# SSD and gMLP layers of a streaming encoder: GpSimd's products move to VectorE, and two tiles of v get banks of their own

## The chip, the core and the metric

The kernel runs on one core of one Trainium2 chip. The metric is the device time of one execution in microseconds (us). The median of three timed runs of the kernel before is 1218.1 us (1212.23 to 1220.72). A difference of about 1% is the least that can be told from no change here.

## The reference

One step of a two-layer streaming encoder, width 1024, on 640 tokens: 512 of one new stream (four tiles of 128 tokens) and 128 of eight running streams (16 tokens each, the fifth tile). All arithmetic is fp32 accurate.

Layer 0 is a Mamba-2 SSD mixer. RMSNorm, then a projection to z, x, B, C and dt; a causal depthwise convolution of width 4 with SiLU on x, B and C; 32 heads of 64 channels in 8 groups that share B and C:

```python
    def step(h, inp):
        la = jnp.cumsum(dtc * a_g, axis=1)
        decay = jnp.exp(jnp.where(causal, seg, -jnp.inf))
        y_in = jnp.einsum('btsg,btsgr,bsgr,bsgrp->btgrp', cb, decay, dtc, xc)
        y_st = jnp.einsum('btgn,bgrpn->btgrp', cc, h) * jnp.exp(la)[..., None]
        w_in = jnp.exp(last[:, None] - la) * dtc
        h_new = h * jnp.exp(last)[..., None, None] + jnp.einsum('bsgn,bsgr,bsgrp->bgrpn', bc, w_in, xc)
```

Then a D skip, a SiLU(z) gate with a group RMSNorm and the output projection, added to the residual. Layer 1 is a gMLP: a projection to u, v and z, GELU on u and v, a LayerNorm of v, for each of 8 head groups a 128x128 position-mixing matrix on v, `u * (W_s v + b) * SiLU(z)`, and an output projection. A final RMSNorm closes it. Outputs are y, the last convolution rows, the new SSM states, and v of the running streams.

## The kernel before

**Precision.** Every fp32 operand of a large matmul is split in a high part (H, rounded) and a low part (L, the rest); three matmuls H·H, H·L and L·H make one product. Splits are made by a ScalarE copy and a VectorE subtraction.

**The weight stream of layer 0.** Weights come in units of 128x1024 fp32 (512 KB). `Stream.fill` (L106) issues on GpSimd's queue the transfer of a unit into `wh` (L112). `Stream.low` (L99) makes the low part of the unit before: ScalarE writes -H into `wl` (L102), and GpSimd issues a second transfer of the same weights that is added to it (L103). `next()` is called before a unit's matmuls and issues the low part of the unit two ahead and the high part of the unit three ahead; each of the two tiles has four buffers. So GpSimd's queue holds, for each unit, L103 and then L112: L103 waits for ScalarE's L102, that waits for the landing of the transfer issued one unit before, and a new L112 stands behind it.

**The SSD groups.** A loop runs over 8 groups (L447). The units of a middle group g (1 to 6), in TensorE's order, are x0, x1, B, C, z0, two of `a_w_out` (o, o, the output projection of group g-1), and z1. x0, x1, B and C are each followed by `conv_tile` (L409), whose last steps are a tanh on ScalarE (L430) and a product on VectorE (L431). `to_tokens` (L467) transposes x to tokens and makes `xdt` (x·dt, VectorE, L481) and `xw` (xdt·decay, GpSimd, L483). `old_states` (L575) reads the running streams' states h0 and then scales them by their decay, eight products on GpSimd (L589). `cb_prompt` (L594) makes `CBm`, the masked C·B (L598); its buffer is shared with `hl`, the split of xw and B that is sent out to DRAM as `dhl`. `mask(i)` (L631) multiplies the four decay tiles E of the group by CBm (L633): three on VectorE and one, the last, on GpSimd; in the last group two and two. `pair(i)` (L635) is the y of two heads. `some(5, 10)` (L704) are the last five of the ten pieces of the output projection, evicted by VectorE (L688). After `pair(1)` come `gate(0)`, `new_states` and the unit z1, then `gate(1)` and in the next group x0 and x1. `gate(i)` (L674) makes tanh (L677), two products (L678, L679), a split (L301 on ScalarE, L302 on VectorE) and a square (L682 on ScalarE); L719 adds the squares of both, and `pss_` (L684) sums them on TensorE during the second half of unit x1. Group 0 has no output projection, and group 7 does the one of group 6 in `L713` to `L718`.

**Order.** In layer 0 TensorE and GpSimd run in the order in which the program is written. VectorE, ScalarE and SyncE run in an order that a planner sets when the program is built; each still runs in order. In layer 1 all engines run in the written order.

**The head of layer 1.** `v_tiles` (L827) makes v in four blocks of 512 columns; tiles 0 to 4 of a block take PSUM banks of the pools `o` and `m` in rotation (L828), ScalarE evicts with GELU (L843), VectorE takes the statistics (L846). `v_norm(t)` (L849) scales a tile by its LayerNorm factors, two ScalarE passes over 1024 columns (L858). Tiles 0 to 2 are scaled in the last block; tiles 3 and 4 in the first step of the loop over 16 feature tiles f (L1015 and L1020). In a step, seven products (`prod`, L957) of 12 matmuls each go to three banks pa (`m`), pb (`in`) and pc (`m`), with evictions between them (L1014 to L1048), and `mix` (L1040) mixes the positions of v. Later work of a step (`gate1`, `gate2`, `new_v`) is put in a list that `then()` takes from between the products of the next step.

Of the kernel before, what the change touches and what calls it, by code (L numbers as in the profile page):

```python
# [12 lines left out]
ALU = mybir.AluOpType  # L13
# [5 lines left out]
TT = 5  # L19
# [21 lines left out]
def hybrid_step(ctx: ExitStack, tc: tile.TileContext, xin, xT0, cst, wdt, cache, wA, wAo, h0in, wB, wBv, wBo,  # L41
                lnwb, spc, bsp, nwb, y_out, nconv_out, sspP_out, sspS_out, v_out):
    nc = tc.nc
    V, S, G, T = nc.vector, nc.scalar, nc.gpsimd, nc.tensor
# [102 lines left out]
    def norm_first(zp, rb):  # L147
        xH, xL = norm_tiles()
        xt = zp.tile([P, KD, NT], F32, name="xt")
        nc.sync.dma_start(out=csb[0][:, :8], in_=cst[:, :8])  # L150
        nc.sync.dma_start(out=xt[:, 0, :], in_=xT0[0])
        dw = zp.tile([P, KD, HEADS], F32, name="dw")
        nc.sync.dma_start(out=dw, in_=wdt)
        dHL = zp.tile([P, KD, 2, HEADS], F32R, name="dHL")
        S.copy(out=dHL[:, :, 0], in_=dw)
        V.tensor_tensor(out=dHL[:, :, 1], in0=dw, in1=dHL[:, :, 0].bitcast(F32), op=ALU.subtract)
        W = stream.first(2, lambda i: [nc.sync.dma_start(out=xt[:, k, :], in_=xT0[k]) for k in ((1,), range(2, KD))[i]])
        nc.sync.dma_start(out=csb[0][:, 8:], in_=cst[:, 8:NCST1])
        acc = [zp.tile([P, NT], F32, name=f"sqa{i}") for i in range(2)]
        for k in range(KD):  # L160
            w = C("nw0")[:, k:k + 1]
            S.activation(xH[:, k, :], xt[:, k, :], AF.Identity, scale=w)
            V.scalar_tensor_tensor(xL[:, k, :], xt[:, k, :], w, xH[:, k, :].bitcast(F32), ALU.mult, ALU.subtract)
        stream.fill(1)
        stream.low()
        warm = ps_op.tile([P, 512], F32, name="warm", tag="op")
        for _ in range(13):
            mm(warm[:, :P], ones, ones)
        pdt, px0 = [[pool.tile([P, 512], F32, name="pin", tag=tag)[:, :b - a] for a, b in HALVES]
                    for pool, tag in ((ps_y, "y"), (ps_in, "in"))]  # L170

        def dt_step(k):
            lw = dHL[:, k].rearrange("p a h -> p (a h)")
            for (a, b), o in zip(HALVES, pdt):
                mm(o[:64], lw, xH[:, k, a:b], start=(k == 0), stop=False)
                mm(o[:64], lw, xL[:, k, a:b], start=False, stop=(k == KD - 1))

        dt_step(0)
        for k in range(KD):
            if k + 1 < KD:  # L180
                dt_step(k + 1)
            for h in range(2):
                in_proj_step(W, (xH, xL), px0[h], h, k)
        dtT = zp.tile([64, NT], F32, name="dtT")
        for (a, b), o in zip(HALVES, pdt):
            S.copy(out=dtT[:, a:b], in_=o[:64])
        for k in range(KD):
            if k < 2:
                S.activation(acc[k], xt[:, k, :], AF.Square, scale=1.0 / 32)
            else:  # L190
                S.activation(xt[:, k, :], xt[:, k, :], AF.Square, scale=1.0 / 32)
                (V if k % 2 else G).tensor_tensor(out=acc[k % 2], in0=acc[k % 2], in1=xt[:, k, :], op=ALU.add)
        V.tensor_tensor(out=acc[0], in0=acc[0], in1=acc[1], op=ALU.add)
        rs = small.tile([P, TT], F32, name="rs0")

        def fin():
            pms = ps_m.tile([P, TT], F32, name="pms", tag="m")
            for t in range(TT):
                mm(pms[:, t:t + 1], acc[0][:, t * P:(t + 1) * P], ones[:, 0:1])
            V.tensor_copy(rs, rsqrt(pms, EPS, TT))  # L200
            ptd = ps_m.tile([P, TT, HEADS], F32, name="ptd", tag="m")
            for t in range(TT):
                mm(ptd[:, t, :], dtT[:, t * P:(t + 1) * P], C("sel")[:64])
            return ptd

        def half(a, b):
            pb = ps_m.tile([P, 512], F32, name="pb", tag="m")
            for t in range(a // P, b // P):
                dg = zp.tile([P, P], F32, name="dg", tag="dg", bufs=2)
                V.tensor_scalar(dg, ident, rs[:, t:t + 1], None, ALU.mult)  # L210
                mm(pb[:, t * P - a:(t + 1) * P - a], ones, dg)
            S.copy(out=rb[:, a:b], in_=pb[:, :b - a])

        return (xH, xL), px0, rs, fin, half
# [77 lines left out]
    def bank(b, n):  # L292
        return {"o": ps_op, "y": ps_y, "m": ps_m}[b].tile([P, 512], F32, name=n, tag={"o": "op"}.get(b, b))
# [29 lines left out]
    with ExitStack() as ca:  # L323
# [35 lines left out]
        for d in (15, 13, 11, 9, 7, 5, 3):  # L359
# [17 lines left out]
                        in1=C("blk").rearrange("p (b o) -> p b o", o=1).broadcast_to([P, 8, HEADS]), op=ALU.mult)  # L377
# [69 lines left out]
        for g in range(GROUPS):  # L447
# [19 lines left out]
            def to_tokens(j, ta, tb):  # L467
                n = tb - ta
                tp = ps_y.tile([P, n, P], F32, name="tp", tag="y")
                for t in range(ta, tb):  # L470
                    T.transpose(out=tp[:, t - ta, :], in_=xcs[j][:, t * P:(t + 1) * P], identity=ident)
                if j == 2:
                    S.copy(out=Bt[:, ta:tb, :], in_=tp)
                    if tb == TT:
                        stack_sample()
                else:
                    xv = tp.rearrange("p t (r q) -> p t r q", q=64)
                    h_ = slice(4 * g + 2 * j, 4 * g + 2 * j + 2)
                    r_ = slice(2 * j, 2 * j + 2)
                    dv = dt[:, ta:tb, h_].rearrange("p t (r o) -> p t r o", o=1).broadcast_to([P, n, 2, 64])  # L480
                    V.tensor_tensor(out=xdt[:, ta:tb, r_], in0=xv, in1=dv, op=ALU.mult)  # L481
                    ev = esu[:, ta:tb, h_].rearrange("p t (r o) -> p t r o", o=1).broadcast_to([P, n, 2, 64])
                    G.tensor_tensor(out=xw[:, ta:tb, r_], in0=xdt[:, ta:tb, r_], in1=ev, op=ALU.mult)  # L483

# [88 lines left out]
            def old_states():  # L575
                Cs = Cf[:, 512:640].rearrange("p (q e j) -> p q e j", q=4, e=2)
                for e in range(2):
                    V.tensor_copy(cz[:, :, e, e, :], Cs[:, :, e, :])
                yq = ps_op.tile([P, 4, 64], F32, name="yq", tag="op")
                for e in range(2):  # L580
                    for q in range(4):
                        mm(yq[32 * q:32 * q + 32], cz[:, q, e].rearrange("p a j -> p (a j)"),
                           h0[q // 2][:, (2 * q + e) % 4], start=(e == 0), stop=(e == 1))
                V.tensor_tensor(out=yss, in0=yq, in1=elt[:, hsl].rearrange("p (r o) -> p r o", o=1).broadcast_to([P, 4, 64]),
                                op=ALU.mult)
                for b in range(8):
                    hv = h0[b // 4][:, b % 4]
                    ev = etot[:, 4 + b, hsl].rearrange("p (r o) -> p r o", o=1).broadcast_to([P, 4, 64])
                    G.tensor_tensor(out=hv, in0=hv, in1=ev, op=ALU.mult)  # L589


            CBm = wk.tile([P, TT, P], F32, name="CBm", tag="CBm", bufs=1)
# [37 lines left out]

            def mask(i):  # L631
                for e in range(2):
                    (G if i and (last or e) else V).tensor_tensor(out=Es[2 * i + e], in0=Es[2 * i + e], in1=CBm, op=ALU.mult)  # L633

            def pair(i):  # L635
                Ms = [Es[2 * i], Es[2 * i + 1]]
# [153 lines left out]
    with ExitStack() as cb_:  # L790
# [34 lines left out]


        def v_tiles(Wv, vb, ts, mid=lambda: None, unit=lambda u: None):  # L827
            pss = [bank("oomm"[(vb * TT + t) % 4], "pv") for t in ts]  # L828
            for u in range(4):
                wH, wL = Wv[u]  # L830
                for t, ps in zip(ts, pss):
# [121 lines left out]
        def then(n=1):  # L953
            for _ in range(min(n, len(later))):
                later.popleft()()
# [32 lines left out]
        for g in range(GROUPS):  # L988
# [9 lines left out]
            for i in range(2):  # L998
# [13 lines left out]
                c5 = wk.tile([P, HT], F32, name="c5", tag="c5", bufs=1)  # L1012
                prod(pa, "m1", True)
                S.copy(out=c1, in_=pa)  # L1014
                if f == 0:  # L1015
                    v_norm(3)
                then()
                prod(pb, "m6", True)
                V.tensor_tensor(out=uu[:, hi], in0=pb, in1=c1, op=ALU.add)
                if f == 0:  # L1020
                    v_norm(4)
                then()
                pc = ps_m.tile([P, 512], F32, name="pqc", tag="m")[:, :HT]
                prod(pc, "m5", True)
# [1 line left out]
                then()  # L1026
                prod(pa, "m2", False)
                S.activation(uu[:, lo], pa, AF.Gelu)
                then()
                prod(pb, "m7", False)  # L1030
                V.tensor_tensor(out=zz[:, hi], in0=pb, in1=c5, op=ALU.add)  # L1031
                then(9)
                prod(pc, "m3", False)
                V.tensor_tensor(out=uu[:, hi], in0=pc, in1=uu[:, hi], op=ALU.add)
# [11 lines left out]
                    mix()  # L1046
                prod(pb, "m4", False)
                V.tensor_tensor(out=zz[:, lo], in0=pb, in1=c1, op=ALU.add)  # L1048
                if not f:
                    mix()  # L1050
                th = wk.tile([P, NT], F32, name="thb", tag="thb", bufs=1)
                S.activation(th, zz, AF.Tanh, scale=0.5)
                qb = wk.tile([P, 2, P], F32, name="qb", tag="qb", bufs=1)
# [23 lines left out]
                    G.tensor_tensor(out=lwb[:, 0], in0=lwb[:, 0], in1=lwb[:, 1], op=ALU.add)  # L1077
                    nc.sync.dma_start(out=v_out[:, f // 4, vs], in_=lwb[:, 0])

                positions()  # L1080
                later.extend([gate1, gate2, new_v])

        oo = bp.tile([P, TT + 2, D], F32, name="oo", tag="v")
        fnw_sb = oo[:, TT]
# [131 lines left out]
```

## Time and profile before

| what | value |
|---|---|
| median of 3 timed runs | 1218.1 us (1212.23 to 1220.72) |
| the profiled execution | 1213.09 us |
| its span, first to last instruction | 1211.3 us |
| mean granted TensorE clock | 0.954 of 2.4 GHz |
| TensorE busy | 1061.1 us (88%) |
| VectorE busy | 838.5 us (69%) |
| ScalarE busy | 451.7 us (37%) |
| GpSimd busy | 200.0 us (17%) |

In the rows PE is TensorE's matmuls, PEld its weight loads, DVE VectorE, ACT ScalarE, POOL GpSimd, SP SyncE. Times are us from the span's start unless they are marked ns. `out<-in` names the tiles that an instruction writes and reads, `L302` is line 302 of the kernel. In a timeline the bracket is the idle time of the engine before the instruction and what ended it. Layer 0 lasts until about 730 us, the rest is layer 1.

### The profile page before, as it was taken

What the parts mean: (1) busy time and instruction counts of PE and PEld (TensorE: products, weight loads), DVE (VectorE), ACT (ScalarE), POOL (GpSimd) and SP (SyncE); (2) the same over time, 40 slices, a digit from 0 to 9 for tenths busy, and PEclk for the clock granted to TensorE, in tenths of its full rate; (3) what the DMA queues carried; (4) which work ended last, traced back from release to release, by engine and by line L of the source; (5) the groups of instructions that cost most, each with busy time, mean ns of one, the idle gap of its engine ahead of it and who ended that gap; (6) DMA issues with size and microseconds to landing.
All of it is one profiled execution on the core that took longest, in us unless ns stands there. A gap on an engine that the chain in (4) does not pass through costs nothing.

```text
span 1211.3 us, 16913 instructions
## 1 busy us (share of the span) xinstructions
PE 1061.1 (88%) x6387; PEld 950.9 (79%) x6387; DVE 838.5 (69%) x1565; ACT 451.7 (37%) x897; POOL 200.0 (17%) x278
## 2 busy tenths in 40 slices
PE   8996887888888887887888888999799999999996
PEld 7885777777777677776777766888789899889985
DVE  6667774675665674665665677664788888888886
ACT  5443515315215215215215224334533343333343
POOL 3123221222232132132132500000000000000000
PEclk9998888989988999998989998999999999999999
DMA  8577647557656656656647551222141333224222
GB/s 271 119 223 197 165 121 200 132 120 200 146 120 192 145 122 189 152 125 180 146 127 187 136 178 64 70 70 78 48 126 62 96 99 104 67 84 126 75 68 87
DMA packets 66001, 157.93 MB, mean 130 GB/s; under 512 B 10080, under 2 KB 28768, under 8 KB 65920
## 3 DMA queue, kind: packets, MB, share of 16 engines
q0 software_dynamic: 18144, 66.07, 24.3%
q1 hardware_dynamic: 47776, 90.78, 24.1%
q8 instruction: 51, 0.84, 0.3%
q14 instruction: 30, 0.25, 0.1%
HBM read 139.96 MB, written 16.86 MB: 129 GB/s over the span
## 4 chain that ended last, share of the span: by engine, by line
PE 29%; issue 23%; DVE 18%; DMA 14%; POOL 8%; ACT 7%; SPq 0%; POOLq 0%; ACTq 0%; DVEq 0%
PE pv L69 8%; PE pop L69 8%; DMA wh<-wA 4%; DMA wh<-wAo 4%; PE pqb L69 3%; DMA dhl<-hl 3%; POOL h L589 3%; DVE wf L751 3%; PE pin L69 2%; PE pqc L69 2%; PE pqa L69 2%; POOL wl L103 2%; POOL wh L112 2%; DVE acc L424 2%; DVE h L967 1%
## 5 line engine op out<-in xcount | busy, mean ns | idle before, releaser
L69 PE MATMUL pin<-xH,wh 128*128 128x384 f32 (+1 forms) x768 | 256.6, 334 | 22.2 <-DVE xp L416 17.7
L69 PE MATMUL pin<-xH,wl 128*128 128x384 f32 (+1 forms) x768 | 244.8, 319 | 1.4 <-DMA wl<-wA 1.4
L69 PE MATMUL pin<-xL,wh 128*128 128x384 f32 (+1 forms) x768 | 245.0, 319 | 0.0
L69 PEld LDWEIGHTS pin<-xH,wh 128*128 128x128 f32 x768 | 153.1, 199 | 32.4 <-issue 24.4
L102 ACT ACTIVATE wl<-wh 128x1024 fp32r<-128x1024 f32 x63 | 66.5, 1056 | 264.6 <-DMA wh<-wA 142.8
L69 PEld LDWEIGHTS pin<-xH,wl 128*128 128x128 f32 x768 | 152.3, 198 | 2.0 <-DMA wl<-wA 2.0
L69 PEld LDWEIGHTS pin<-xL,wh 128*128 128x128 f32 x768 | 153.5, 200 | 0.2
L69 PE MATMUL pop<-wh,yHL 128*128 128x512 f32 x320 | 104.8, 409 | 19.3 <-DVE CBm L598 10.0
L424 DVE SCALAR_TENSOR_TENSOR acc<-xp,cw,acc 128x664 f32<-128x664 f32 x96 | 91.8, 956 | 37.6 <-ACT acc L419 36.1
L69 PE MATMUL pop<-wf,yHL 128*128 128x512 f32 x480 | 115.3, 397 | 1.4 <-DVE h L967 0.7
L69 PEld LDWEIGHTS pop<-wf,yHL 128*128 128x128 f32 x480 | 89.2, 188 | 25.4 <-DVE h L967 3.7
L751 DVE TENSOR_TENSOR wf<-raw,wf 128x512 fp32r<-128x512 f32 x128 | 86.6, 686 | 28.1 <-ACT wf L750 27.1
L103 POOL DMA_DIRECT2D wl<-wA x47 | 41.5, 883 | 348.4 <-ACT wl L102 315.7
L750 ACT CAST wf<-raw 128x512 fp32r<-128x512 f32 x128 | 76.5, 616 | 56.8 <-PE pop L69 27.2
L69 PEld LDWEIGHTS pop<-wh,yHL 128*128 128x128 f32 x320 | 58.0, 190 | 36.3 <-DVE CBm L598 12.1
L431 DVE SCALAR_TENSOR_TENSOR xc<-xc,acc 128x512 f32<-128x512 f32 x64 | 28.7, 489 | 61.0 <-ACT xc L430 60.8
L69 PE MATMUL pqa<-xH,wf 128*128 128x320 f32 x256 | 63.7, 318 | 5.3 <-ACT v L843 3.2
L688 DVE SCALAR_TENSOR_TENSOR h<-pop,rr,h 128x512 f32<-128x512 f32 x80 | 59.4, 746 | 10.3 <-PE pop L69 9.9
L69 PE MATMUL pv<-wh,xL 128*128 128x512 f32 x160 | 63.4, 396 | 2.4 <-DVE xL L235 2.4
L69 PE MATMUL pqb<-tf,wf 128*128 128x320 f32 x384 | 63.0, 313 | 2.0 <-DVE zz L1031 2.0
L69 PE MATMUL pv<-wh,xH 128*128 128x512 f32 x160 | 63.5, 397 | 0.1
L69 PE MATMUL pv<-wl,xH 128*128 128x512 f32 x160 | 63.1, 395 | 0.0
(223 smaller groups left out, 2067.9 us busy)
## 6 DMA issues: line engine op xcount, KB each, us to landing
wh<-wA POOLq DMA_DIRECT2D x47, 512.0 KB, 7.2
wl<-wA POOLq DMA_DIRECT2D x47, 512.0 KB, 5.6
raw<-wB SPq DMA_DIRECT2D x32, 512.0 KB, 3.7
E<-laD SPq DMA_DIRECT2D x32, 320.0 KB, 8.5
h<-h0in SPq DMA_DIRECT2D x16, 512.0 KB, 5.0
out_sspS<-h SPq DMA_DIRECT2D x16, 512.0 KB, 5.4
wh<-wAo POOLq DMA_DIRECT2D x16, 512.0 KB, 6.5
wl<-wAo POOLq DMA_DIRECT2D x16, 512.0 KB, 5.7
```

The costliest lines, as they stand in the source:

```text
L69: T.matmul(out, lhsT=lhsT, rhs=rhs, start=start, stop=stop, **kw)
L102: S.activation(L, H.bitcast(F32), AF.Identity, scale=-1.0)
L103: G.dma_start(out=L, in_=src, accum_op=ALU.add)
L112: G.dma_start(out=H, in_=src)
L424: V.scalar_tensor_tensor(acc[:, 0:664], xp[:, k:k + 664], cw[:, 4 * ft + k:4 * ft + k + 1], acc[:, 0:664], ALU.mult, ALU.add)
L431: V.scalar_tensor_tensor(o, o, 1.0, a, ALU.add, ALU.mult)
L589: G.tensor_tensor(out=hv, in0=hv, in1=ev, op=ALU.mult)
L688: V.scalar_tensor_tensor(h1[:, t, dsl], ps, rg[:, t:t + 1], h1[:, t, dsl], ALU.mult, ALU.add)
L750: S.copy(out=t[:, 0], in_=src)
L751: V.tensor_tensor(out=t[:, 1], in0=src, in1=t[:, 0].bitcast(F32), op=ALU.subtract)
L967: V.scalar_tensor_tensor(h1[:, t, dsl], ps, 0.5, h1[:, t, dsl], ALU.mult, ALU.add)
```

## The change

Five things:

- The three sums of squares in `norm_first` (L192) that GpSimd made are made by VectorE.
- `xw` (L483), the eight state decays of a group (L589) and all masks (L633) are made by VectorE. GpSimd has only the issues of weight transfers left in layer 0.
- Tiles 3 and 4 of v take the two banks of the pool `y`, the others `o`, `o` and `m`, the same in every block.
- `v_norm(3)` and `v_norm(4)` are written two products later each: after the GELU of pa's second use, and after L1031.
- The mixing of step f = 0 is no longer at the end of its own step but in the list of later work, with the rest of its positions, so it runs between the products of step 1.

```diff
@@ norm_first @@
-                (V if k % 2 else G).tensor_tensor(out=acc[k % 2], in0=acc[k % 2], in1=xt[:, k, :], op=ALU.add)
+                V.tensor_tensor(out=acc[k % 2], in0=acc[k % 2], in1=xt[:, k, :], op=ALU.add)
@@ to_tokens @@
-                    G.tensor_tensor(out=xw[:, ta:tb, r_], in0=xdt[:, ta:tb, r_], in1=ev, op=ALU.mult)
+                    V.tensor_tensor(out=xw[:, ta:tb, r_], in0=xdt[:, ta:tb, r_], in1=ev, op=ALU.mult)
@@ old_states @@
-                    G.tensor_tensor(out=hv, in0=hv, in1=ev, op=ALU.mult)
+                    V.tensor_tensor(out=hv, in0=hv, in1=ev, op=ALU.mult)
@@ mask @@
-                    (G if i and (last or e) else V).tensor_tensor(out=Es[2 * i + e], in0=Es[2 * i + e], in1=CBm, op=ALU.mult)
+                    V.tensor_tensor(out=Es[2 * i + e], in0=Es[2 * i + e], in1=CBm, op=ALU.mult)
@@ v_tiles @@
-            pss = [bank("oomm"[(vb * TT + t) % 4], "pv") for t in ts]
+            pss = [bank("oommyy"[t + 1 if t > 2 else t], "pv") for t in ts]
@@ the loop over feature tiles @@
                 prod(pa, "m1", True)
                 S.copy(out=c1, in_=pa)
-                if f == 0:
-                    v_norm(3)
                 then()
                 prod(pb, "m6", True)
                 V.tensor_tensor(out=uu[:, hi], in0=pb, in1=c1, op=ALU.add)
-                if f == 0:
-                    v_norm(4)
                 then()
...
                 prod(pa, "m2", False)
                 S.activation(uu[:, lo], pa, AF.Gelu)
+                if f == 0:
+                    v_norm(3)
                 then()
                 prod(pb, "m7", False)
                 V.tensor_tensor(out=zz[:, hi], in0=pb, in1=c5, op=ALU.add)
+                if f == 0:
+                    v_norm(4)
                 then(9)
...
                 V.tensor_tensor(out=zz[:, lo], in0=pb, in1=c1, op=ALU.add)
-                if not f:
-                    mix()
...
-                positions()
-                later.extend([gate1, gate2, new_v])
+                if f:
+                    positions()
+                    later.extend([gate1, gate2, new_v])
+                else:
+                    later.extend([gate1, lambda m=mix, p=positions: (m(), p()), gate2, new_v])
```

## Rows read from the trace of the kernel before

**Rows 1.** Busy time of PE, PEld, DVE, ACT, POOL from 253 to 342, clock, DMA
```profile
253.00:342.00 89.00, 74.37 (x477) 66.65 (x476) 54.77 (x103) 31.06 (x68) 22.26 (x31) 0.94 0.62 154
```

**Rows 2.** Waits of TensorE, all of the span: total us, times, longest
```profile
PE yB L69 <- POOL E L633: 29.5, 6, 4.9
...
PE pin L69 <- DVE xp L416: 17.7, 5, 4.7
...
PE pop L69 <- DVE y L654: 4.7, 1, 4.7
...
PE pqa L69 <- ACT v L843: 3.2, 1, 3.2
...
PE pqb L69 <- DVE zz L1031: 2.0, 1, 2.0
```

**Rows 3.** Chain that ended last, 240 to 345: start, us, what
```profile
253.29 4.56 POOL h L589 x8
...
263.61 8.38 issue
```

**Rows 4.** Timeline of GpSimd, from the last pop of group 2 on
```profile
252.69 0.55 POOL L112 DMA_DIRECT2D wh<-wA  x1 [11.82 <-PE pop L69]
...
262.17 0.89 POOL L103 DMA_DIRECT2D wl<-wA  x1 [2.83 <-ACT wl L102]
```

**Rows 5.** Timeline of VectorE in the same stretch
```profile
253.93 6.09 DVE L302 SCALAR_TENSOR_TENSOR yHL<-y,csb,yHL 128x640 fp32r<-128x640 f32 x1
...
275.09 0.88 DVE L302 SCALAR_TENSOR_TENSOR yHL<-y,csb,yHL 128x640 fp32r<-128x640 f32 x1 [0.90 <-ACT yHL L301]
...
284.45 0.82 DVE L719 TENSOR_TENSOR y<-y 128x640 f32<-128x640 f32 x1 [8.01 <-ACT y L682]
...
327.37 0.69 DVE L598 TENSOR_TENSOR CBm<-cb,csb 128x512 f32<-128x512 f32 x1 [4.18 <-DMA dhl<-hl]
```

**Rows 6.** Groups by shape, whole span: busy us, mean ns, idle before
```profile
L302 DVE SCALAR_TENSOR_TENSOR yHL<-y,csb,yHL 128x640 fp32r<-128x640 f32 x16 | 45.4, 2837 | 13.1 <-ACT yHL L301 13.1
```

**Rows 7.** Timeline of ScalarE in the same stretch
```profile
260.06 0.74 ACT L682 ACTIVATE y<-y 128x640 f32<-128x640 f32 x1 [6.64 <-DVE yHL L302]
260.70 1.04 ACT L102 ACTIVATE wl<-wh 128x1024 fp32r<-128x1024 f32 x1
...
282.74 1.06 ACT L102 ACTIVATE wl<-wh 128x1024 fp32r<-128x1024 f32 x1 [7.68 <-DMA wh<-wA]
```

**Rows 8.** The transfer issued at 252.69: KB, us from issue to landing
```profile
wh<-wA POOLq DMA_DIRECT2D x1, 512.0 KB, 3.8
```

**Rows 9.** Products of the same shapes on VectorE
```profile
L633 DVE TENSOR_TENSOR E<-E,CBm 128x640 f32<-128x640 f32 x23 | 19.9, 875 | 0.1
...
L481 DVE TENSOR_TENSOR xdt<-tp,dt 128x512 f32<-128x512 f32 x16 | 10.9, 684 | 0.6 <-DMA laD<-laT 0.4 <-PE tp L471 0.2
...
L567 DVE TENSOR_TENSOR hs<-hs,etot 128x256 f32<-128x256 f32 x24 | 10.3, 428 | 4.1 <-ACT hs L564 3.8
```

**Rows 10.** TensorE from 258 to 264: length, busy (matmuls), granted clock, DMA share, GB/s
```profile
258.00:264.00 6.00, 4.61 (x26) 0.52 0.09 8
```

**Rows 11.** The products on GpSimd, by shape
```profile
L589 POOL TENSOR_TENSOR h<-h,etot 128x256 f32<-128x256 f32 x64 | 37.3, 651 | 1.0 <-PE yq L69 0.9
L483 POOL TENSOR_TENSOR xw<-xdt,esu 128x512 f32<-128x512 f32 x16 | 24.7, 1546 | 57.4 <-DVE xdt L481 57.4
L633 POOL TENSOR_TENSOR E<-E,CBm 128x640 f32<-128x640 f32 x9 | 15.2, 1688 | 3.7 <-issue 3.7
```

**Rows 12.** Timeline of VectorE in group 1: the C·B mask
```profile
148.06 0.68 DVE L598 TENSOR_TENSOR CBm<-cb,csb 128x512 f32<-128x512 f32 x1
```

**Rows 13.** Timeline of GpSimd in group 7, after the two masks
```profile
692.86 0.90 POOL L103 DMA_DIRECT2D wl<-wAo  x1
```

**Rows 14.** Timeline of ScalarE in group 7
```profile
685.57 1.06 ACT L102 ACTIVATE wl<-wh 128x1024 fp32r<-128x1024 f32 x1 [6.67 <-DMA wh<-wAo]
...
701.51 1.06 ACT L102 ACTIVATE wl<-wh 128x1024 fp32r<-128x1024 f32 x1 [7.44 <-DMA wh<-wAo]
```

## The prediction

> **What bounds the kernel now.** I read the busy times by stretch first. In a middle SSD group of 89 us TensorE works 74.4, VectorE 54.8 and GpSimd 22.3 us [rows 1]: no engine is full, so layer 0 is bound by waits, not by an engine. The waits of TensorE name them: six times yB waits 4.9 us for the one mask that GpSimd makes (29.5 us), five times unit x1 waits for VectorE's L416 (17.7 us), once a pop waits 4.7 us [rows 2]. The chain that ended last then passes, in each group, through GpSimd: the eight state decays, the mask, and the issues of the weight stream with the landings between them [rows 3]. All this has one form at the six ends of groups 1 to 6; I take that of group 2. T is 252.69, when the last pop frees a buffer and GpSimd can issue the high part of x1 [rows 4].
>
> Until T GpSimd stands 11.8 us at that issue [rows 4], and the decays and the mask are written behind it. So the mask, whose inputs are long there, comes only after the issue, the 4.6 us of the decays [rows 3] and its own time, and TensorE waits for it. In the same 6 us VectorE's split L302 takes 6.09 us, while the same instruction takes 0.88 at 275.09 [rows 5]. Over the kernel, 16 of them take 45.4 us [rows 6]; 16 at 0.88 are 14.1, the excess of 31.3 is six times 5.2. L302 holds the square L682 on ScalarE until 260.06, and behind that in ScalarE's order stands L102, the low part of x1, at 260.70 = T + 8.0 [rows 7]. Its weights had landed at T + 3.8 [rows 8]. From L102 the stream goes on: GpSimd's next two issues at T + 9.5 [rows 4], landing, L102, issue. The third such L102 comes at 282.74, waiting 7.7 us for its landing [rows 7]; behind it stands the square of gate(1), behind that L719 on VectorE (8.0 us idle, 284.45) [rows 5], and behind that L416, which frees the bank for x1's second half. So between T and T + 33 it is the stream, not TensorE, that sets the pace, and TensorE's wait for the mask is partly slack.
>
> **The boundary of two groups, six times.** The mask on VectorE costs 0.87 [rows 9], is written ahead of five evictions and is ready some 7 us before T: yB's wait goes. L302 is back at 0.88, so the square ends at about T + 2.9, and L102 of x1 can start when its weights land, at T + 3.8 plus a few tenths. It moves from T + 8.0 to T + 4.0. TensorE gains more, 4.9 us of wait, and also some of what it lost at a granted clock of 0.52, the lower of its two levels (1.2 GHz), after that wait [rows 10], but it runs into the stream: x1's second half waits for the third L102, which moved by 4.0 only. So the wait of L416 grows from 3.4 to some 5.5 us, and what the boundary gains is 4.0 us. Ends: 0 (the landings eat it) and 4.9 plus the 3.5 us of L416's wait (17.7 over 5), if that goes too. I take 4.0, since every later step hangs on that L102. Six times: 24.0.
>
> **What VectorE gets.** For each group eight decays like L567 at 0.43, 3.4 us; one mask (two in group 7); and four pieces of xw like L481, two at 0.68 and two smaller ones, at most 2.7 us [rows 9]. On GpSimd they took 0.65, 1.69 and 1.55 each [rows 11]. The decays are ready once the old states are read, just before L598, the C·B mask. There VectorE stands 4.2 us for the transfer of `hl` that holds the shared buffer [rows 5]: 3.4 fits in the hole, and costs nothing. Without that cover, 3.4 us would go straight onto the masks and pops of the group. In group 1 there is no hole, L598 runs without idle before it [rows 12]: a loss of 0 to 4.3. Against it, GpSimd's issues in groups 0 and 1 no longer stand behind xw and the decays (0 to 4). I take 0 for both together. The second mask of pair 1 stands before the evictions of the late pops; they run behind TensorE by less than a piece there, and I take 0, at most 0.9 a group. xw lies beside waits of VectorE for ScalarE's tanh, taken as 0, at most 2.7 a group. The three sums of squares: 0, from -1 to +1; VectorE has them done when TensorE comes to the sum.
>
> **Group 7.** GpSimd makes two masks there, and the issue L103 at 692.86 stands behind them [rows 13], though its L102 ended at 686.6 [rows 14]. The next high part then lands at 701.5, ScalarE waits 7.4 us for it [rows 14], with gate(0)'s split behind it, and in the end a pop waits 4.7 us [rows 2]. Without the masks the issue goes 5.9 us earlier. The gain ends at TensorE's wait: 4.7, ends 2 and 5.9.
>
> **The head of layer 1.** Product m1 waits 3.2 us for the GELU of tile 4, whose bank it takes [rows 2]. The new banks remove that, but m2 must wait for ScalarE's copy of pa, which stays where it is: TensorE gets there earlier and waits longer, gain 0. m4 waits 2.0 us for L1031 [rows 2], held by the scaling of tiles 3 and 4 on ScalarE; later scaling gives up to 2.0, and step 1 pays part of it. In the first block tiles 3 and 4 now wait until the transposes of the norm have left the `y` banks: a loss of up to 2. I take a gain of 1, ends -3 and +4.
>
> **The sum.** 24.0 + 0 + 4.7 + 1.0 = 29.7. Against the profiled execution, 1213.1 - 29.7 = 1183.4 us. The median of the runs stands 5.0 above that execution, so for a median **1188 us**, chance 0.62.
>
> **A rule beside the trace.** The L302 rows say that one VectorE instruction stood through nine instructions of GpSimd. The Trainium skill (SBUF — State Buffer, Who interferes with whom) says that a VectorE instruction with two SBUF inputs and a GpSimd instruction that reads SBUF exclude each other, and that the second to issue blocks until the first finishes. The trace agrees that they exclude each other, but it shows a wait of 5.2 us, not one of a single GpSimd instruction. By the letter of that rule only the first 0.65 us of the wait were GpSimd's.
>
> **Rivals.**
> 1. *The long L302 has another cause, and stays.* Then L102 of x1 stays at T + 8.0, TensorE loses in front of x1 what it gains at yB, and the boundaries give 0: 1213.1 - 4.7 - 1.0 = 1207.4, as a median 1212. For it: the wait is longer than one GpSimd instruction. Against it: it is there only beside GpSimd's products, six times the same 5.2 us. Chance 0.07.
> 2. *The landings eat half.* With TensorE 5 us earlier, SyncE's loads of states and decays fall earlier on the stream, and the later landings (7.7 us of idle at 282.74 [rows 7], against 3.8 us alone [rows 8]) stretch. At 2 us a boundary: 1213.1 - 12 - 4.7 - 1 = 1195.4, median 1200. Chance 0.17.
> 3. *Both waits go.* The planner lets the square of gate(1) go ahead of the third L102, so x1 does not wait: 29.5 + 17.7 + 4.7 + 1 = 52.9, median 1165. For it: VectorE's, ScalarE's and SyncE's order is planned anew. Against it: nothing in the change alters what that square and that L102 wait for. Chance 0.08.
> 4. *Slower: VectorE becomes the bound of the SSD groups.* Place: the stretch from the conv products to the masks. The added 3.4 + 0.9 + 2.7 = 7.0 us a group lie on its path, over 8 groups 56, against the gain of 29.7: 1213.1 + 26 = 1239, median 1244. It decides where the hole ahead of L598 is under 3.4 us, or the planner puts the decays behind L598 in all groups. For it: group 1 has no hole. Against it: 54.8 of 89 us busy, of which 5.2 was standing in L302. Chance 0.06.
>
> **How the numbers follow.** 1% of 1218 is 12, about what can be told from no change, so faster is below 1206 and slower above 1230. Forecast (0.62), rival 3 (0.08) and most of rival 2 (0.12 of 0.17) are faster: 0.82. Rival 1 and the rest of 2 are within: 0.12. Rival 4: 0.06. The range reaches from 1170, which takes in the upper ends of the forecast's terms, to 1213, with rivals 1 and 2, and leaves out 3 and 4.
>
> **What would show it.** L302 at 0.88 in all 16; no wait of yB for a mask; L102 of x1 at about T + 4.0; the wait of x1 for L416 grown to 5 us or more at five or six boundaries; L598 still idle before it in groups 2 to 7, with the decays in that hole. The forecast is wrong if the third L102 comes no earlier after T than 30.0 us, if the decays stand behind L598, or if L416's wait shrinks.

## The result and the profile after

The changed kernel takes 1198.3 us (median of 4 runs, 1195.4 to 1201.4) against 1217.4 for the kernel before on the same chip: a ratio of 0.985 [0.980, 0.989], 19 us less. The forecast was 1188, inside 1170 to 1213. The profiled execution has a span of 1198.9 against 1211.3; of these 12.4 us layer 0 gives 18.2 (the first matmul on `pv` moves from 734.0 to 715.8) and layer 1 takes 5.9 back. These two are single executions, and lie closer together than the medians.

What the prediction said of instructions is there. VectorE's split, the evictions ahead of it and the product behind T, from the timeline of VectorE after (T is now 253.66), and the group by shape:

```profile
254.25 0.75 DVE L688 SCALAR_TENSOR_TENSOR h<-pop,rr,h 128x512 f32<-128x512 f32 x1 [0.54 <-PE pop L69]
254.92 0.88 DVE L302 SCALAR_TENSOR_TENSOR yHL<-y,csb,yHL 128x640 fp32r<-128x640 f32 x1
```
```profile
L302 DVE SCALAR_TENSOR_TENSOR yHL<-y,csb,yHL 128x640 fp32r<-128x640 f32 x16 | 14.1, 880 | 8.4 <-ACT yHL L301 8.4
```

All 16 are short, against 45.4 us [rows 6]. The stream follows on ScalarE, L102 being the negation that waits for a landing:

```profile
257.26 1.06 ACT L102 ACTIVATE wl<-wh 128x1024 fp32r<-128x1024 f32 x1 [0.70 <-DMA wh<-wA]
267.96 1.06 ACT L102 ACTIVATE wl<-wh 128x1024 fp32r<-128x1024 f32 x1 [9.63 <-DMA wh<-wA]
...
273.18 0.74 ACT L682 ACTIVATE y<-y 128x640 f32<-128x640 f32 x1 [0.95 <-DVE yHL L302]
281.03 1.06 ACT L102 ACTIVATE wl<-wh 128x1024 fp32r<-128x1024 f32 x1 [7.11 <-DMA wh<-wA]
```

The first L102 comes at T + 3.6 (before T + 8.0 [rows 7]), but the third at T + 27.4 (before T + 30.1): 1.7 of the 4.4 us are lost on the way, in waits of 9.6 and 7.1 for landings. In the mean of the six boundaries 2.9 of 4.3 us are lost by then. The square of gate(1), L682, now stands ahead of the third L102, not behind it. The waits of TensorE, whole span, after:

```profile
PE tp L471 <- DVE xc L431: 44.0, 12, 6.3
PE pin L69 <- DVE xp L414: 34.0, 13, 4.8
PE pqa L69 <- ACT c L1014: 7.2, 2, 5.5
...
PE tp L471 <- DVE xdt L481: 5.8, 1, 5.8
PE pqc L69 <- DVE c L1021: 4.9, 4, 2.4
...
PE yB L69 <- DVE E L633: 2.0, 6, 0.4
...
PE pop L69 <- DVE y L654: 0.4, 1, 0.4
```

The same two groups that lead this list, in the kernel before:

```profile
PE tp L471 <- DVE xc L431: 27.4, 15, 6.6
...
PE pin L69 <- DVE xp L414: 3.8, 1, 3.8
```

yB's 29.5, L416's 17.7 and group 7's 4.7 [rows 2] are gone or nearly so (2.0, none and 0.4); in their place L414 has grown by 30 us and xc by 17, the evictions and the conv of the next tile.

### The profile page after: what moved, and what is told of

The parts are those of the page before. It is cut to its first block, busy times and chain, and to the rows that moved or that the text cites. A ratio compares the mean times of both kernels' runs of the same rounds, so it can differ in the third digit from the quotient of the medians.

```text
span 1198.9 us, 16816 instructions
## 1 busy us (share of the span) xinstructions
PE 1063.2 (89%) x6387; PEld 958.0 (80%) x6387; DVE 830.3 (69%) x1673; ACT 453.9 (38%) x897; POOL 110.5 (9%) x170
## 4 chain that ended last, share of the span: by engine, by line
issue 49%; PE 25%; DVE 13%; POOL 7%; ACT 4%; DMA 2%; SPq 0%; POOLq 0%; ACTq 0%; DVEq 0%
PE pv L69 9%; PE pop L69 5%; PE pqb L69 4%; POOL wh L112 4%; POOL wl L103 3%; PE pqa L69 3%; PE pqc L69 3%; DVE wf L751 2%; DVE h L967 1%; DMA wh<-wA 1%; DVE uu L1062 1%; ACT wf L750 1%; DVE thb L1061 1%; DVE uu L1065 1%; ACT yHL L298 1%
## 5 line engine op out<-in xcount | busy, mean ns | idle before, releaser
L69 PE MATMUL pin<-xH,wh 128*128 128x384 f32 (+1 forms) x768 | 259.7, 338 | 35.6 <-DVE xp L414 34.0
L102 ACT ACTIVATE wl<-wh 128x1024 fp32r<-128x1024 f32 x63 | 66.7, 1059 | 248.6 <-DMA wh<-wA 184.9
L424 DVE SCALAR_TENSOR_TENSOR acc<-xp,cw,acc 128x664 f32<-128x664 f32 x96 | 87.0, 906 | 92.8 <-ACT acc L419 91.5
L751 DVE TENSOR_TENSOR wf<-raw,wf 128x512 fp32r<-128x512 f32 x128 | 86.5, 686 | 29.4 <-ACT wf L750 28.3
L471 PE MATMUL tp<-csb,xc 128*128 128x128 f32 x120 | 27.9, 345 | 53.3 <-DVE xc L431 44.0
L471 PEld LDWEIGHTS tp<-csb,xc 128*128 128x128 f32 x120 | 18.7, 177 | 58.5 <-DVE xc L431 34.2
```

The lines of the kernel that those rows point to most:

```text
L69: T.matmul(out, lhsT=lhsT, rhs=rhs, start=start, stop=stop, **kw)
L102: S.activation(L, H.bitcast(F32), AF.Identity, scale=-1.0)
L424: V.scalar_tensor_tensor(acc[:, 0:664], xp[:, k:k + 664], cw[:, 4 * ft + k:4 * ft + k + 1], acc[:, 0:664], ALU.mult, ALU.add)
L751: V.tensor_tensor(out=t[:, 1], in0=src, in1=t[:, 0].bitcast(F32), op=ALU.subtract)
```

## The experiments

Twelve kernels, each against the kernel before. T is the issue that waited for the last pop, as in the prediction; the first and last of six are listed, a period is a fifth of their distance. Differences in us that the text gives for a kernel are its ratio's, times the median of before (1211.5 to 1217.4). Layer 1 runs from the first matmul on `pv` to the last on `pqa`.

| kernel | ratio to before [95%] | first, last T | period | third L102 after T, mean | layer 1 begins, lasts |
|---|---|---|---|---|---|
| before | 1 | 162.63, 611.64 | 89.8 | 29.6 | 734.0, 430.9 |
| the change | 0.985 [0.980, 0.989] | 165.39, 602.39 | 87.4 | 28.2 | 715.8, 436.8 |
| 1 masks alone | 0.996 [0.993, 0.999] | 161.56, 612.81 | 90.3 | 31.8 | 731.1, 430.3 |
| 2 decays alone | 0.991 [0.987, 0.996] | 162.32, 600.20 | 87.6 | 28.6 | 720.2, 430.9 |
| 3 masks and decays | 0.978 [0.974, 0.982] | 161.50, 594.23 | 86.5 | 28.1 | 708.0, 429.9 |
| 4 head alone | 1.006 [1.003, 1.008] | 166.09, 617.60 | 90.3 | 29.4 | 738.4, 436.6 |
| 5 change without head | 0.982 [0.978, 0.986] | 163.24, 600.05 | 87.4 | 28.2 | 714.2, 430.0 |
| 6 (3) with banks | 0.978 [0.974, 0.982] | 161.82, 595.00 | 86.6 | 28.1 | 708.4, 431.4 |
| 7 (6) with own memory | 0.982 [0.978, 0.985] | 165.28, 599.75 | 86.9 | 28.2 | 715.2, 431.9 |
| 8 (3), negation on GpSimd | 1.008 [1.005, 1.011] | 166.65, 624.41 | 91.6 | 30.2 (on GpSimd) | 745.2, 430.8 |
| 9 before, issue later | 1.018 [1.015, 1.022] | 170.51, 643.03 | 94.5 | 28.1 | 758.9, 430.0 |
| 10 (3) without stores | 0.962 [0.958, 0.966] | 163.74, 574.42 | 82.1 | 24.3 | 685.5, 429.6 |
| 11 (3), high part first | 0.923 [0.920, 0.927] | 151.62, 537.08 | 77.1 | 16.7 | 642.7, 430.0 |
| 12 before, high part first | 0.941 [0.938, 0.943] | 151.83, 554.71 | 80.6 | 28.2 | 664.9, 431.4 |

Layer 1's length is steady (429.6 to 431.9 in all kernels without the late scaling). The periods are nearly so: 3, 6 and 7 have the same code in layer 0 and lie within 0.4 us, before and 4 differ by 0.5. The first T is not: 6 and 7 differ by 3.5 us there, before and 4 as well. A difference of single executions in layer 0 counts here where the period shows it too, and by more than 0.5 us.

Each kernel gets a new order from the planner, so no experiment changes its edit alone. The square L682 of gate(1) stands behind the third L102 in the kernel before and in experiment 2, and ahead of it in 1, 3 and the change.

### The parts of layer 0

**Experiment 1, masks alone.** Edit in `mask`:

```diff
-(G if i and (last or e) else V).tensor_tensor(out=Es[2 * i + e], ...
+V.tensor_tensor(out=Es[2 * i + e], ...
```

> The kernel before, with only GpSimd's masks (the second mask of pair 1, and both in group 7) moved to VectorE. The eight state decays and xw stay on GpSimd. Theory A (what the boundary gains goes through L302: VectorE's split stands while GpSimd works off the decays that queue behind the transfer issued at T, and holds the square, L102 and with it the stream): the six waits of yB for the mask go, 29.5 us, but L302 still takes about 5.2 us (nine GpSimd products become eight), L102 of x1 comes at T + 6.4 instead of T + 8.0, and TensorE waits that much longer for L416 in front of x1's second half. Gain 1 to 1.6 us a boundary and up to 4.7 in group 7: 8 to 14 us less than before. Rival B (the mask is what TensorE waited for, the rest is incidental): most of the whole change is here already, 16 to 20 us less than before.

5 us less, below theory A's 8 to 14. The first L102 comes at T + 6.5, as theory A has it, and L302 is still long (VectorE by shape):

```profile
L302 DVE SCALAR_TENSOR_TENSOR yHL<-y,csb,yHL 128x640 fp32r<-128x640 f32 x16 | 36.5, 2279 | 8.5 <-ACT yHL L301 8.5
```

TensorE's longest waits:

```profile
PE tp L471 <- DVE xc L431: 40.6, 18, 6.1
PE pin L69 <- DVE xp L414: 33.2, 7, 6.0
```

The period is no shorter at all, and the third L102 comes 2.2 us later after T: the 29.5 us of yB and the 17.7 of L416 came back at L414 (33.2, from 3.8) and xc (40.6, from 27.4). Rival B falls: TensorE's largest wait was not what it lost by.

**Experiment 2, decays alone.** Edit in `old_states`: `G.tensor_tensor(out=hv, ...)` becomes `V.tensor_tensor(out=hv, ...)`.

> The kernel before, with only the eight state decays per group moved to VectorE. The masks and xw stay on GpSimd. Theory A: behind the issue at T stands one product only, the mask of 1.5 us, so the mask is ready at T + 2.1 and yB waits under 1 us; L302 takes about 2.4 us, the square ends near T + 4.4 and L102 of x1 comes at T + 4.5 to 5. Gain of the boundary 1.5 to 2 us, six times, and nothing in group 7: 8 to 13 us less than before. Rival B: the mask is 4.6 us earlier, which gives most of yB's 29.5 us: 16 us or more less than before. Rival C (VectorE pays for the decays, since they now stand straight in front of L598 with no idle time left between): about 2.5 us a group lost, the gain is under 3 us or there is none.

11 us less, in theory A's range; L102 at T + 3.5 to 3.9, a little earlier than it said; yB waits 2.3 us in six for GpSimd's mask and 4.4 in ten for VectorE's. With L102 early and the square behind the third L102 as it was, L416 now holds TensorE for 39.5 us in six waits. Rival C, which had VectorE pay for the decays, falls.

**Experiment 3, both edits.**

> The kernel before, with masks and decays moved to VectorE; xw stays on GpSimd. Theory A: L302 at 0.88 in all 16, L102 of x1 at T + 3.6, the boundary gain of the whole change, 2.4 us, six times, and the 4.7 of group 7, less what groups 0 and 1 lose (0 to 2.8): 14 to 19 us less than before, so that xw and the head are worth -2 to +3 together. Rival C: with the decays on VectorE it is slower than with the masks alone.

26 us less, more than theory A had, more than the sum of 1 and 2 (16), and 8 us better than the whole change: the rest of it costs. How much of the 10 us above that sum is owed to the planner's order, which differs between 2 and 3, was not separated. Rival C falls for good. The period is 3.3 us shorter; from the last T to layer 1 it takes 113.8 against 122.4.

**Experiment 5, the change without the head of layer 1** (3, with xw and the sums of squares on VectorE too).

> The changed kernel without its change at the head of layer 1: masks, decays, xw and the sums of squares on VectorE. Against masks and decays alone (26 us less than before) it has the four pieces of xw more. Theory X (xw is not free on VectorE: its pieces stand ahead of the next tile's L414 and delay the evictions that unit needs; the trace of the changed kernel has 34 us of waits for L414 against 14 with masks and decays alone): 4 to 8 us slower than masks and decays alone, 18 to 22 us less than before. Rival H (xw is hidden, and all that the whole change lacks against masks and decays alone is lost at the head of layer 1): within 2 us of masks and decays alone, 24 to 28 us less than before.

22 us less, in theory X's range. The time does not separate 5 from 3: their intervals overlap, and experiment 7, without xw, has the ratio of 5. The period does, though by little more than its scatter: 87.4 here and in the whole change, 86.5 to 86.9 in 3, 6 and 7. VectorE in the stretch where C's first half is evicted, in the whole change and then in 3:

```profile
308.05 0.89 DVE L431 SCALAR_TENSOR_TENSOR xc<-xc,acc 128x512 f32<-128x512 f32 x2 [2.24 <-ACT xc L430]
308.86 0.28 DVE L483 TENSOR_TENSOR xw<-xdt,esu 128x128 f32<-128x128 f32 x1
309.06 0.55 DVE L414 TENSOR_TENSOR xp<-pin,rb 128x384 f32<-128x384 f32 x1
```
```profile
300.70 0.55 DVE L414 TENSOR_TENSOR xp<-pin,rb 128x384 f32<-128x384 f32 x1
303.79 0.89 DVE L431 SCALAR_TENSOR_TENSOR xc<-xc,acc 128x512 f32<-128x512 f32 x2 [2.55 <-ACT xc L430]
```

With xw to place, the planner put L414 behind L431 and a piece of xw. L431 waits for ScalarE's tanh, and that stands behind an L102 which waited for TensorE. ScalarE in the whole change:

```profile
306.44 1.06 ACT L102 ACTIVATE wl<-wh 128x1024 fp32r<-128x1024 f32 x1 [4.64 <-PE pin L69]
```

So the next unit of TensorE stands 3.9 us for L414 at 309.67. In experiment 5 the order is the same and the wait 3.3. The 10.0 us that TensorE waits for the C·B mask in experiment 3 are 0.7 here, so a period loses only some 0.5 to 0.9. In group 0 the wait for xdt grows from 2.4 to 5.2 besides; the first T, which scatters by 3.5, does not show it.

### The head of layer 1

**Experiment 4, the head alone.** The diff of `v_tiles` and of the loop over feature tiles, on the kernel before.

> The kernel before, with only the head of layer 1 changed: banks of their own for the last two tiles of v, their scaling later, gate and positions reordered in the first step. Layer 0 is as before. My sum has a gain of 1 us (ends -3 and +4): m1's wait of 3.2 us goes, m2's wait for the copy of pa grows by as much, m4's wait halves. Rival D (the head carries more of the gain than the boundaries): 5 us or more less than before.

7 us more. Layer 1 takes 5.7 us longer; the expectation had a loss of 3 at most, and rival D a gain.

**Experiment 6, the banks without the later scaling and mixing.**

```diff
-pss = [bank("oomm"[(vb * TT + t) % 4], "pv") for t in ts]
+pss = [bank("oommyy"[t + 1 if t > 2 else t], "pv") for t in ts]
```

> Masks and decays on VectorE, and of the head of layer 1 the banks alone: the last two tiles of v in banks of their own, scaling, mixing and positions where they were. Theory L (the banks are neutral, the later scaling and mixing cost): m1 no longer waits 3.2 us, but the copy of pa stands behind rsb's copy, which cannot start until L905 has ended, so that m2's wait grows to 5.5 us; the first blocks lose 0.9 us to the transposes: 0 to +1 us against masks and decays alone, that is 25 to 26 us less than before. Rival K (the banks cost, by the y banks that the transposes need): 4 to 6 us slower than masks and decays alone.

The same ratio as experiment 3, layer 1 longer by 1.5: theory L holds, the banks are neutral, and of the 5.7 to 5.9 us some 5 (436.8 - 431.4) belong to the later scaling and mixing. The first two steps show where. From the first copy of pa (L1014) to the third it takes 31.2 us in 3 (836.13 to 867.34), 32.2 in 6 (837.47 to 869.64) and 36.0 in the whole change (845.74 to 881.73), so 3.8 us of it against the kernel with the same banks. In step 1 of the whole change TensorE waits 1.7 us for the copy of pa, 1.0 for L1017 and 2.4 for L1021. The copy stands on ScalarE behind the tanh of the step before (L1050), which waited for VectorE; the late scaling had ended 5.7 us ahead of it and is not what holds it. L1021 stands on VectorE behind the moved positions. That the scaling costs at all, beside the moved mixing and positions, is not shown.

**Experiment 7, rsb and c1 in memory of their own.**

```diff
-rsb = wk.tile(...)
+rsb = bp.tile(...)
-c1 = wk.tile(...)
+c1 = bp.tile(...)
```

> As the kernel with the banks alone, and rsb and c1 lie in the pool bp, in memory of their own, not in the pool opened after the one whose tile L905 reads. Theory L: the two copies no longer wait for L905, m2 starts when the copy of pa is done, and its wait falls from 5.5 to under 2 us: 3 to 4 us less than the banks alone, 28 to 30 us less than before. Rival M (it is not that memory that holds the copies, or VectorE's next additions L1019 and L1025, which stand behind L905 in its order, hold TensorE at the next product): no more than 1 us less than the banks alone.

No gain. TensorE in step 0, with the banks alone and then with the copies moved:

```profile
837.96 0.63 PE L69 MATMUL pqa<-xH,wf 128*128 128x320 f32 x1 [5.53 <-ACT c L1014]
```
```profile
840.91 0.41 PE L69 MATMUL pqa<-xH,wf 128*128 128x320 f32 x1 [1.17 <-ACT c L1014]
847.16 0.63 PE L69 MATMUL pqb<-xH,wf 128*128 128x320 f32 x1 [4.23 <-DVE uu L1019]
```

It was that memory that held the copy, and the second half of rival M holds too: the wait moves one product on, to VectorE's L1019.

### What sets the pace

**Experiment 8, the negation on GpSimd.**

```diff
-S.activation(L, H.bitcast(F32), AF.Identity, scale=-1.0)
+G.tensor_scalar(L, H.bitcast(F32), -1.0, None, ALU.mult)
```

> Masks and decays on VectorE, and the negation of the stream's low part (L102) on GpSimd, not on ScalarE, so that ScalarE never stands for a landing. Theory S (what is left of the boundary is ScalarE standing at L102 for landings, 7 to 10 us at the second and third after T, with gate and conv steps behind it): the waits of TensorE for L416, L414 and xc shrink, 10 to 25 us less than masks and decays alone, 36 to 50 less than before. Rival V (a GpSimd product beside VectorE's two-input products makes these stand, as L302 did, and now 60 times for 2 to 3 us, and VectorE is on the path): 5 us or more slower than masks and decays alone. Rival T (TensorE is what ends last there, the standing of ScalarE is covered): within 4 us of it.

10 us slower than before, 36 slower than 3. Of theory S's waits two did go (xc 44.3 to 4.6, L414 14.0 to 3.8), and L416 came back (none to 13.7). That ScalarE's standing at L102 was their cause fits this but is not shown by it, since TensorE itself comes later here. The negation takes 2.85 us on GpSimd, 63 times, against 1.06 on ScalarE, and TensorE now waits for the low parts. Two waits of TensorE and the group on GpSimd:

```profile
PE pin L69 <- DMA wl<-wA: 41.6, 19, 3.3
PE pop L69 <- DMA wl<-wAo: 32.9, 7, 7.2
```
```profile
L102 POOL TENSOR_SCALAR wl<-wh 128x1024 fp32r<-128x1024 f32 x63 | 179.5, 2849 | 370.7 <-issue 205.9 <-PE yq L69 36.4 <-PE yB L69 29.3
```

It is slower, as rival V says, but in another way: VectorE's busy time grows by 19 us only, and the stream itself becomes the bound.

**Experiment 9, the kernel before with the issue behind the products.**

```diff
-Wo = [stream.next(), stream.next()]
+Wo = [stream.next(), stream.next(2)]
+stream.low()
...
 mask(1)
+if 0 < g < GROUPS - 1:
+    stream.fill(3)
```

> The kernel before, with all products where they were, on GpSimd; only the issue of x1's high part (groups 1 to 6) is written behind the decays and the mask, not ahead of them. Theory A (the loss was the queueing of the products behind an issue that stands for a buffer, not GpSimd's slowness): decays and mask run while GpSimd would stand, the mask is ready before T, nothing is on GpSimd beside L302, which takes 0.88, L102 of x1 comes at T + 3.6 to 4; the six boundaries give what they give with masks and decays on VectorE, 3 us each, and group 7 gives nothing: 14 to 22 us less than before, with no product more on VectorE. Rival W (VectorE's two-input instructions stand beside GpSimd's products wherever these run): the pops' evictions ahead of T take the 5 us a group instead, under 8 us less than before.

22 us slower. L102 is at T + 3.8 and L302 short, as theory A has it, yet T itself is later. VectorE and then GpSimd ahead of T (L634 is here the mask L633):

```profile
244.10 6.61 DVE L567 TENSOR_TENSOR hs<-hs,etot 128x256 f32<-128x256 f32 x1
250.63 0.81 DVE L634 TENSOR_TENSOR E<-E,CBm 128x640 f32<-128x640 f32 x1
```
```profile
244.06 4.88 POOL L589 TENSOR_TENSOR h<-h,etot 128x256 f32<-128x256 f32 x8
248.62 1.79 POOL L634 TENSOR_TENSOR E<-E,CBm 128x640 f32<-128x640 f32 x1
```

L567 takes 0.42 elsewhere. Here it stands until GpSimd's ninth product has ended at 250.41, and the pops wait 7.1 us behind it in five groups. Rival W holds, and it is worse than W had it: theory A's "queueing behind the issue" was a wrong reason for a right move, since ahead of the issue the same products cost more. In both places a product of VectorE with two inputs stands beside them; a place without one was not tried.

**Experiment 10, no stores of the new states.** The kernel leaves out the stores of groups 1 to 6, so it shows what they cost and is no substitute.

```diff
+if g in (0, GROUPS - 1):
     nc.sync.dma_start(out=sspS_out[g, i], in_=h0[i])
```

> Masks and decays on VectorE; the stores of the new sample states of groups 1 to 6 (two of 512 KB a group, issued by SyncE some 7 to 16 us after T) are left out. Theory R (SyncE's transfers stretch the landings of the second and third high part after T, which ate most of the 4.4 us that the first L102 gained: the third L102 moved from T + 29.6 to T + 28.1 only): the third L102 comes at T + 25.5 to 27, and each boundary gives 1 to 2 us more: 6 to 12 us less than masks and decays alone. Rival Q (the stream's own transfers, or the loads that now start earlier, fill the time): the third L102 stays at T + 27.5 to 28.5, within 4 us of masks and decays alone.

20 us less than experiment 3. ScalarE after T = 327.97:

```profile
331.54 1.06 ACT L102 ACTIVATE wl<-wh 128x1024 fp32r<-128x1024 f32 x1 [0.67 <-DMA wh<-wA]
342.22 1.06 ACT L102 ACTIVATE wl<-wh 128x1024 fp32r<-128x1024 f32 x1 [9.62 <-DMA wh<-wA]
352.92 1.06 ACT L102 ACTIVATE wl<-wh 128x1024 fp32r<-128x1024 f32 x1 [4.74 <-DMA wh<-wA]
```

The third L102 is 3.8 us earlier after T than in 3, and the period 4.4 shorter: SyncE's transfers do stretch the third landing, more than theory R said. The second L102 does not move (T + 14.6 in the mean, 14.4 in 3). Nor are the stores alone in this: in 3 SyncE issues them at T + 6.8 and T + 15, with the loads of the next states and decays from T + 14.4 on; here these loads go out from T + 6.8 on. In the kernel before the first store goes out at T + 13.7 to 14.8 and the loads from T + 19 on, so masks and decays on VectorE brought SyncE's transfers forward by some 4 to 7 us, into the time of the second and third landing, as rival 2 of the prediction has it. What the stores cost the kernel before was not run.

**Experiment 11, the high part first.** In `Stream.fill`:

```diff
-    self.low()
     src, = self.srcs[len(self.got)]
     ...
     G.dma_start(out=H, in_=src)
+    self.low()
```

> Masks and decays on VectorE; in the weight stream the high part of the next unit is issued ahead of the low part of this one, so that a landing of a high part no longer waits for ScalarE's negation of the one before. Theory S (the chain L103, landing, L102 sets the pace between T and T + 30): the second L102 moves from T + 14.4 to T + 8 to 11, the third from T + 28.1 to T + 20 to 25, 5 to 15 us less than masks and decays alone. Rival T (a high part that stands for a buffer holds the low part of the unit before it, which then lands too late): TensorE waits for wl, and it is slower than masks and decays alone by 5 us or more.

1120 us, 93 less than before and 67 less than experiment 3, where theory S had 5 to 15. GpSimd after T (L111 is here the issue L112):

```profile
304.96 0.55 POOL L111 DMA_DIRECT2D wh<-wA  x1 [18.59 <-PE pop L69]
305.59 0.88 POOL L103 DMA_DIRECT2D wl<-wA  x1
306.14 0.88 POOL L111 DMA_DIRECT2D wh<-wA  x1
310.69 0.87 POOL L103 DMA_DIRECT2D wl<-wA  x1 [3.67 <-ACT wl L102]
```

Two high parts go out within 1.2 us of T, where each had waited for the landing and negation of the one before. The second and third L102 come at T + 10.0 and T + 16.7 in the mean. Theory S counted the boundaries alone; the period, 77.1, is 9.5 shorter than in 3, the first T comes 9.9 earlier, and the stretch from the last T to layer 1 is 8.2 shorter. L414 holds TensorE once, 3.9 us, L416 and the C·B mask no more, and xc still 37.8. Rival T, that the low part now held by a buffer would be late, does not show.

**Experiment 12, the same order on the kernel before.**

> The kernel before, all its products on GpSimd, with the order of the stream alone changed: the high part of the next unit is issued ahead of the low part of this one. With masks and decays on VectorE this order took the time from 26 us to some 92 us less than before. Theory P (the price of GpSimd's products does not hang on the stream: after T VectorE's split stands for the decays and the mask, and yB waits for the mask): L302 long six times, yB's wait 4 to 8 us six times; the order alone gives 50 to 70 us, and 20 to 40 us lie between this kernel and the one with masks and decays on VectorE too. Rival N (what the change gained it gained only by the stream's first L102, so with a fast stream masks and decays may lie anywhere): within 10 us of the kernel with both, 82 to 92 us less than before.

72 us less than before, just over what theory P gave the order alone; 21 us (0.941 - 0.923 of 1212) still lie between it and 11. TensorE's wait and VectorE's split are as in the kernel before, or worse:

```profile
PE yB L69 <- POOL E L633: 35.0, 6, 5.8
```
```profile
L302 DVE SCALAR_TENSOR_TENSOR yHL<-y,csb,yHL 128x640 fp32r<-128x640 f32 x16 | 50.9, 3184 | 11.1 <-ACT yHL L301 11.1
```

So masks and decays are worth 21 to 26 us with either stream, as theory P has it.

## Why the prediction came out as it did

**The boundaries: right up to the first L102, short behind it.** L302, L102 and yB's wait went where the text put them. It took 4.0 us a boundary; experiment 3, which has only the edits meant, shows 3.3, and the whole change 2.4. The step "every later step hangs on that L102", so that its 4.0 us carry over, is the one that failed in its size. In experiment 3 the first L102 after T comes 4.3 us earlier than before, the second 3.2, the third 1.5 and the fourth 3.2 again (means of six): the landings, beside transfers of SyncE that had moved forward too, ate 2.8 of the 4.3 (experiment 10), and 1.7 came back at the fourth unit. Which step gave it back is open. Rival 2 named these landings, with 2 us a boundary and 1200 us. That 1198 lies so close to its 1200 is luck: the landings cost less than it had, and the head of layer 1, with xw, cost the rest.

L416's wait did not grow but went, as rival 3 had it, since the planner let the square go ahead of the third L102. Where the square stayed behind (experiment 2), the wait grew, to 39.5 us in six. The gain of rival 3 did not follow: the wait reappeared at L414 and xc. That L416's wait would shrink was one of the three signs named for a wrong forecast; the text had said that nothing in the change alters this order.

**Group 7: right.** With the sixth boundary it was forecast at 8.7 us; from the last T to layer 1 experiment 3 gains 8.6 and the whole change 9.0. The two shares were not separated.

**xw: too low.** It was taken as 0, lying beside waits of VectorE, with 2.7 a group as the end. By the period it cost 0.5 to 0.9 a group, close to the scatter, and the order shows how: it pushed L414 out of its place on VectorE.

**The decays: right in experiment 3, not shown in the change.** In 3 they fit into the hole ahead of L598, which keeps 1.6 to 2.6 us of idle in groups 2 to 7. In the whole change L598 has no idle time before it in any group, so the sign "L598 still idle before it" fails there; the decays do stand ahead of it, and TensorE waits 0.2 us for that mask.

**The head of layer 1: wrong in sign.** It was +1 with ends -3 and +4; it is -5.9. That m1's wait turns into m2's was right (5.53 us). The step that failed is "later scaling gives up to 2.0, and step 1 pays part of it": the wait for zz falls from 2.0 to 0.9, and the first two steps become 3.8 us longer than with the banks alone.

So the sum of 29.7 is in experiment 3 as 26, and the head and xw, at first 1 and 0, take 7 of it away again. The time stayed inside the range because that reaches 25 us above the forecast, for rivals 1 and 2; neither had a loss in layer 1.

## What to carry over

Before an engine's busy time or its longest wait, look for the in-order chain that feeds it: here GpSimd issue, landing, ScalarE's negation, next issue, one weight unit at a time, set the pace of layer 0, and exchanging two lines of it was worth more than three times what the change was. Removing TensorE's largest wait alone gave 5 us; the wait came back further on, behind the same chain. A move called free for its engine must be checked for what it displaces in that engine's order.

## What the runs showed of the hardware

A VectorE product with two inputs in SBUF, issued beside GpSimd's eight decays, stood until the last of them had ended, and until the mask behind them had where there was one: 6.61 us for L567 beside nine products (experiment 9), 6.09 for L302 beside nine [rows 5], 4.61 beside eight (experiment 1). Beside the mask alone L302 took 1.56 (experiment 2). Not every run does this. In group 7 of the kernel before GpSimd makes two masks in a row, and a mask of VectorE comes to its end between them (GpSimd, then VectorE):

```profile
688.71 2.12 POOL L633 TENSOR_TENSOR E<-E,CBm 128x640 f32<-128x640 f32 x1 [3.69 <-issue]
690.79 2.13 POOL L633 TENSOR_TENSOR E<-E,CBm 128x640 f32<-128x640 f32 x1
```
```profile
689.35 2.15 DVE L633 TENSOR_TENSOR E<-E,CBm 128x640 f32<-128x640 f32 x1
```

VectorE's ends at 691.50, 0.67 after GpSimd's first, and GpSimd's second takes 2.13 where the same mask takes 1.52 in group 2. Why VectorE gets its turn here and not among the decays is open. With GpSimd's one-input negation (experiment 8) two of the sixteen L302 ran inside one, and took 1.05 and 0.99. By the Trainium skill (SBUF — State Buffer, Who interferes with whom) one of the two blocks while the other's instruction holds the shared ports; the exclusion agrees, and so does the turn between the two masks, but the wait for all eight decays is more than that sentence gives.
